# S5 tables planned without a margin, and the scans of an S5 half in two groups with their output products

## The chip, the cores and the metric

The kernel runs on one core of one Trainium2 chip. The metric is device time in microseconds (us). TensorE is called PE here, its weight loads PEld, VectorE DVE, ScalarE ACT, GpSimd POOL and SyncE (which issues the DMAs) SP.

## The reference

Two layers are applied to x, 1024 positions of 1024 channels. Each normalises, projects to nine pieces, runs three mixers on them, gates the result and projects it back:

```
for l in range(DEPTH):                       # DEPTH = 2
    h = rms_norm(x, norm_w[l])
    fq, fk, fv, flog, su, rq, rk, rv, gate = split_cols(h @ w_in[l])
    y_fox = forgetting_attention(fq, fk, fv, log_sigmoid(flog + fox_b_f[l]))
    y_s5  = s5_layer(su, ...)                # 16 groups of 16 channels, 64 complex states
    y_ret = retention(rotary(rq), rotary(rk), rv, ret_gn_w[l])   # 4 heads
    x = x + (concat(y_fox, y_s5, y_ret) * silu(gate)) @ w_out[l]
return rms_norm(x, final_norm_w)
```

The S5 layer is a complex linear recurrence over the positions, x_t = λ x_{t−1} + B u_t, read out by y = Re(C x) + d u, then GELU and a gate. λ and B come from a_re, a_im, b_re, b_im and log_dt by elementwise work on small tables, exp, cos and sin among it.

## The kernel before

PE computes in single precision by three products of split halves (XH·wh, XL·wh, XH·wl), which is why a projection is always a run of 8 + 8 + 8 matmuls of 128x512. Weights arrive as wr; ACT casts them to wh and DVE makes the rest wl.

**S5.** A layer first builds tables (`s5_tables`, `s5_bc`, then `s5_half_tables` for each of two halves of eight groups). PE transposes the rows of a (s5ab) and of c (s5cn); DVE makes powers of λ (s5pw, s5e) and a matrix s5R; PE multiplies s5cc with s5R and transposes s5R, and the results go to DRAM as the matrices s5Bs, s5Cs, s5D and the factors s5Er, s5Ei. Later `s5_half` (L865) works on one half: it loads them and the channels s5U, PE makes Bs·U for two groups of four (ps_s), ACT copies the swapped half out (s5bs, two copies a group), DVE multiplies by Er, POOL the swapped copy by Ei, and DVE subtracts (s5b). Then come eight scans on DVE, s5z along the positions. For the read-out ACT makes swapped copies s5zs, DVE multiplies z by Er, POOL zs by Ei, DVE adds, and PE adds up D·U and Cs·z in ps_s; the GELU follows.

**Retention.** `ret_chain` runs over eight blocks: PE makes scores (ps_s), DVE decays them (rsd) and the state (x), rotated keys are transposed (rkt), PE adds into ps_o, DVE copies to ro. Every two blocks `ret_norm` normalises: ACT squares (rsq), DVE reduces (rvar) and takes an inverse root in small steps (rry, rrt, rrh), scales ro, and PE transposes ro twice two times, which ACT takes out with the weight (ry). The rotation of queries and keys (rot, rsw) is made by ACT copies, two POOL products by cosine and sine, and a DVE sum.

**What sets the order.** The program is written by a planner, the class `Weave`. Each part is a generator thread with a priority and a margin. At `yield need(...)` a thread states what its next step waits for. The planner keeps a clock for PE and takes, in order of priority, the first thread whose inputs are ready, by its own estimate plus the margin, at that clock; it then writes all instructions up to the thread's next `need` into the program. A margin therefore delays a step in PE's order, so that its inputs are surely there. The margins stand in `SLACK` (L29): s5 2.0 us, tab 5.0 us for the tables, rn 3.0, ret 0.5. The order on the other engines is taken by a scheduler that follows this program order and the dependences. Every engine executes its instructions strictly in that order: an instruction that waits holds up all behind it. Every operation is issued through one helper, so the rows of the profile all show its line, L158, and are told apart by their tiles.

PSUM tiles are few: two for projections (ps_proj), three for ps_s, two for ps_t, one for ps_o. A PE step that needs a ps_s waits until the oldest has been read.

`s5_all_tables` (L852) is the thread of the tables; `trunk` adds it for layer 0 at the start, with priority 1, and for layer 1 near the end of layer 0, with priority 5, both with the margin tab.

Of the kernel before, what the change touches and what calls it, by code (L numbers as in the profile page):

```python
# [13 lines left out]
ALU = mybir.AluOpType  # L14
# [14 lines left out]
SLACK = dict(s5=2.0, ret=0.5, rn=3.0, tab=5.0, fox=0.4, val=1.0)  # L29
# [135 lines left out]
def need(*tiles, ps=(), ev=()):  # L165
    return tiles, ps, ev
# [3 lines left out]
def hybrid_block(ctx: ExitStack, tc: tile.TileContext, a: dict, out: bass.AP, taps=None):  # L170
# [4 lines left out]
    W = Weave(PSUM)  # L175
    V, S, G, PE = (Clocked(W, k, e) for k, e in (("V", nc.vector), ("S", nc.scalar), ("G", nc.gpsimd), ("P", nc.tensor)))
# [565 lines left out]
    def s5_bc(l):  # L742

        bb, cc = (slot("pt", [128, 2, 16, 16], F32, n) for n in ("s5bb", "s5cc"))
        B1, B2, C1, C2 = bb[:, 0], bb[:, 1], cc[:, 0], cc[:, 1]
        dma(out=B1[0:64], in_=a["s5_b_re"][l].rearrange("g p h -> p g h"))
        dma(out=B1[64:128], in_=a["s5_b_im"][l].rearrange("g p h -> p g h"))
        V.tensor_scalar(out=B2[0:64], in0=B1[64:128], scalar1=-1.0, scalar2=None, op0=ALU.mult)
        V.tensor_copy(out=B2[64:128], in_=B1[0:64])
        cn = slot("p", [128, 2, 2, 64], F32, "s5cn")  # L750
        for j, nme in enumerate(("s5_c_re", "s5_c_im")):
            dma(out=cn[:, :, j, :], in_=a[nme][l].rearrange("(x g) h p -> (g h) x p", x=2))
        yield need(cn, ps=("t",))
        pt = psum("t", (128, 2, 128))
        for x in range(2):
            PE.transpose(pt[:, x, :], cn[:, x].rearrange("c j p -> c (j p)"), ident)
        V.tensor_copy(out=C1[0:64].rearrange("p (x g) h -> p x (g h)", x=2), in_=pt[0:64])
        V.tensor_scalar(out=C1[64:128].rearrange("p (x g) h -> p x (g h)", x=2), in0=pt[64:128], scalar1=-1.0, scalar2=None, op0=ALU.mult)
        V.tensor_copy(out=C2[0:64], in_=C1[64:128])
        V.tensor_scalar(out=C2[64:128], in0=C1[0:64], scalar1=-1.0, scalar2=None, op0=ALU.mult)  # L760
        return B1, B2, C1, C2
# [90 lines left out]
    def s5_all_tables(l, tag, box, before, mid, hold):  # L852
        yield need(ev=before)
        T = yield from s5_tables(l)
        BC = yield from s5_bc(l)
        box["rho"] = T["rho"]
        W.add(s5_late_tables(l, T, BC), 6)
        yield need(ev=mid)
        for hf in range(2):
            yield from s5_half_tables(l, hf, T, BC, tag, hold[hf])  # L860
            W.done.add(("early", l, hf))

    tanh = [None]

    def s5_half(l, hf, rho):  # L865
        sh = [128, 8, 128]
        tb = tb_d[l, hf]

        def load(j, name):
            t = slot("qb", sh, F32, name)  # L870
            dma(out=t, in_=tb[j])
            return t

        U = slot("qb", sh, F32, "s5U")
        Bs = load(4, "s5Bs")
        dma(out=U, in_=ud_d[hf])
        Er, Ei = load(0, "s5Er"), load(1, "s5Ei")

        D = slot("qb", sh, F32, "s5D")
        kv = kd_d[hf]  # L880
        dma(out=D, in_=bass.AP(kv.tensor, kv.offset, [[16, 8], [1920, 16], [240, 8], [1, 128]]))
        b, bs, z = (slot("p", sh, F32, n) for n in ("s5b", "s5bs", "s5z"))
        for q in range(2):
            gq = slice(q * 4, q * 4 + 4)
            yield need(Bs, U, ps=("s",))
            ps = psum("s", (128, 4, 128))
            for g in range(4):
                PE.matmul(ps[:, g, :], lhsT=Bs[:, q * 4 + g, :], rhs=U[:, q * 4 + g, :], start=True, stop=True)
            S.copy(out=bs[0:64, gq], in_=ps[64:128])
            S.copy(out=bs[64:128, gq], in_=ps[0:64])  # L890
            V.tensor_tensor(out=b[:, gq], in0=ps, in1=Er[:, gq], op=ALU.mult)
            G.tensor_tensor(out=bs[:, gq], in0=bs[:, gq], in1=Ei[:, gq], op=ALU.mult)
            V.tensor_tensor(out=b[:, gq], in0=b[:, gq], in1=bs[:, gq], op=ALU.subtract)
        Cs = load(3, "s5Cs")
        for g in range(8):
            gg = hf * 8 + g
            V.tensor_tensor_scan(out=z[:, g, :], data0=rho[:, gg:gg + 1].to_broadcast([128, 128]), data1=b[:, g, :],
                                 initial=0.0, op0=ALU.mult, op1=ALU.add)
        zs, Y = (slot("p", sh, F32, n) for n in ("s5zs", "s5Y"))
        for q in range(2):  # L900
            gq = slice(q * 4, q * 4 + 4)
            S.copy(out=zs[0:64, gq], in_=z[64:128, gq])
            S.copy(out=zs[64:128, gq], in_=z[0:64, gq])
            V.tensor_tensor(out=z[:, gq], in0=z[:, gq], in1=Er[:, gq], op=ALU.mult)
            G.tensor_tensor(out=zs[:, gq], in0=zs[:, gq], in1=Ei[:, gq], op=ALU.mult)
            V.tensor_tensor(out=z[:, gq], in0=z[:, gq], in1=zs[:, gq], op=ALU.add)
            yield need(z, D, Cs, ps=("s",))
            ps = psum("s", (128, 4, 128))
            for g in range(4):
                gi = q * 4 + g  # L910
                PE.matmul(ps[:, g, :], lhsT=D[:, gi, :], rhs=U[:, gi, :], start=True, stop=False)
                PE.matmul(ps[:, g, 1:128], lhsT=Cs[:, gi, :], rhs=z[:, gi, 0:127], start=False, stop=True)
            S.copy(out=Y[:, gq], in_=ps)

            if q == 0:
                e = slot("p", sh, F32, "s5q")
            S.activation(out=e[:, gq], in_=Y[:, gq], func=AF.Square)
            V.tensor_scalar(out=e[:, gq], in0=e[:, gq], scalar1=0.044715, scalar2=1.0, op0=ALU.mult, op1=ALU.add)
            V.tensor_tensor(out=e[:, gq], in0=e[:, gq], in1=Y[:, gq], op=ALU.mult)
            tanh[0] = S.activation(out=e[:, gq], in_=e[:, gq], func=AF.Tanh, scale=GELU_C)  # L920
            V.scalar_tensor_tensor(out=Y[:, gq], in0=e[:, gq], scalar=1.0, in1=Y[:, gq], op0=ALU.add, op1=ALU.mult)
        dma(out=yd_d[hf], in_=Y)
        W.done.add(("s5h", l))
# [316 lines left out]
    def trunk():  # L1240
        raws = rv_load(0)
        load_x(range(2, NT))
        dma(out=ct, in_=a["c_tab"])
        zt = slot("v", [32, 8, 112], F32, "zt")
        V.memset(zt, 0.0)
        dma(out=kd_d[:, :, :, 0:7, :].rearrange("q c g l h -> (q c) g (l h)"), in_=zt)
        W.add(first_norm(), 0)
        rvw = rv_split(raws, normed[1].ins)
        box = {}
        W.add(s5_all_tables(0, "qb", box, (("xt", 0, 6),), (), ((("su", 0, 1, 0),), (("su", 0, 1, 1),))), 1, SLACK["tab"])  # L1250
        for l in range(depth):
            last = l == depth - 1
            rv = [slot("v", [128, 4, 256], F32, "rv") for _ in range(2)]
            fl = small([128, NT, 8], F32, "fl", 1)
            yield from rv_flog(l, rvw, rv, fl)
            W.add(forget_gates(l, fl), 2)
            U = []
            W.add(s5_chain(l, box), 1, SLACK["s5"])
            W.add(ret_chain(l, U, rv), 2, SLACK["ret"])
            jobs = su_jobs(l, ("qb", "qb") if l else ("qa", "qa")) + rot_jobs(l, U)  # L1260
            for p in range(4):
                tiles = {}
                js = fox_jobs(l, p, tiles)

                def start_k(start=js[3][1], p=p, tiles=tiles):
                    W.add(fox_attend(l, p, tiles), 3)
                    return start()

                jobs += js[:3] + [(js[3][0], start_k, *js[3][2:])]
            c0, c1 = {}, {}  # L1270
            W.add(out_weights(l, 0, c0, (("att", l, 2),)), 4)
            yield from granules(jobs, [gate_job(l, 2), gate_job(l, 3)], [gate_job(l, 0), gate_job(l, 1)])
            src = x_src if l == 0 else x1_d
            W.add(out_weights(l, 1, c1, (("att", l, 3),)), 4)
            if not last:
                box = {}
                W.add(s5_all_tables(l + 1, "qa", box, (("att", l, 3),), (("c0", l),), ((("c1", l, 1),), (("c1", l, 3),))), 5, SLACK["tab"])
            yield from out_first(l, c0, src)
            nw = load_bc("nc", a["final_norm_w"] if last else a["norm_w"][l + 1])
            if not last:  # L1280
                rvw = rv_split(rv_load(l + 1))
            yield from out_second(l, c1, src, nw, last)
# [52 lines left out]
```

## Time and profile before

| | |
|---|---|
| median of three runs | 1197.11 us (1195.18 to 1197.67) |
| the profiled execution | 1195.99 us, its span 1194.3 us |
| PE busy | 1150.3 us, 96% |
| DVE busy | 887.2 us, 74% |
| ACT busy | 543.5 us, 46% |
| POOL busy | 193.6 us, 16% |
| mean granted clock of PE | 0.989 of 2.4 GHz |

The span runs from the first to the last instruction. A granted clock of 1.00 in a stretch is 2.4 GHz; the lower level is 1.2 GHz. In a row of the trace the first number is the start, the second the time from the start of the first to the end of the last instruction of a merged run; brackets hold the idle time of the engine ahead of it and the instruction that ended it. Ends of matmuls overlap the starts of the next, so runs of matmuls are measured from start to start.

### The profile page before, as it was taken

The page shows a single profiled execution, that of the slowest core. Times are in us where ns is not written, and L with a number is a line of the kernel's source. Part 1 is how long each engine was busy: PE and PEld are TensorE (multiplying, and loading weights), DVE is VectorE, ACT ScalarE, POOL GpSimd, SP SyncE. Part 2 cuts the span into 40 slices and gives each one's busy share as a digit, 9 for nine tenths or more (in the row PEclk, how much of TensorE's full clock was granted, in tenths as well). Part 3 has the DMA queues.
Part 4 walks back from the last instruction along what each step waited for, and adds up shares of the span by engine and source line. Part 5 has one row for each costly group of instructions (what it writes and reads, how often), then busy time and mean ns, then how long its engine had stood idle before and what let it go on. Part 6 is the DMA issues. An engine that isn't in the chain of part 4 may idle for free. (4 is left out here: it accounts for less than half of the span.)

```text
span 1194.3 us, 18899 instructions
## 1 busy us (share of the span) xinstructions
PE 1150.3 (96%) x6320; PEld 978.8 (82%) x6320; DVE 887.2 (74%) x2555; ACT 543.5 (46%) x1061; POOL 193.6 (16%) x439
## 2 busy tenths in 40 slices
PE   8899898999999999999999999999999999999997
PEld 7878687878788788987789888877888878898885
DVE  7798886577777678885878938765876868788645
ACT  6436414345555456543243355344544545555312
POOL 0016301121121221200000153111212112121000
PEclk9999999999999999999899999999999999999998
DMA  7157316642405225936241833454352331475524
GB/s 236 40 144 204 109 54 176 168 168 73 122 27 132 73 54 157 305 127 208 90 147 56 256 92 92 112 159 142 115 133 62 89 106 45 133 234 195 181 97 159
DMA packets 147204, 157.44 MB, mean 132 GB/s; under 512 B 20833, under 2 KB 109601, under 8 KB 147106
## 3 DMA queue, kind: packets, MB, share of 16 engines
q1 hardware_dynamic: 147104, 156.22, 44.0%
q8 instruction: 50, 0.82, 0.3%
q14 instruction: 48, 0.39, 0.1%
q10 hardware_dynamic: 2, 0.00, 0.0%
HBM read 99.13 MB, written 40.29 MB: 117 GB/s over the span
## 5 line engine op out<-in xcount | busy, mean ns | idle before, releaser
L158 PE MATMUL ps_proj<-XH,wh 128*128 128x512 f32 (+1 forms) x864 | 228.3, 391 | 4.9 <-DVE ql L158 2.5
L158 PE MATMUL ps_proj<-XL,wh 128*128 128x512 f32 (+1 forms) x864 | 229.7, 391 | 0.0
L158 PE MATMUL ps_proj<-XH,wl 128*128 128x512 f32 (+1 forms) x864 | 223.3, 387 | 0.5 <-DVE wl L158 0.5
L158 PEld LDWEIGHTS ps_proj<-XH,wh 128*128 128x128 f32 x864 | 155.6, 189 | 35.5 <-DVE ql L158 2.9
L158 PEld LDWEIGHTS ps_proj<-XH,wl 128*128 128x128 f32 x864 | 155.8, 188 | 30.3 <-DVE wl L158 1.0
L158 PEld LDWEIGHTS ps_proj<-XL,wh 128*128 128x128 f32 x864 | 156.7, 190 | 28.8
L158 PE MATMUL ps_proj<-wo,XH 128*128 128x512 f32 x512 | 162.8, 393 | 0.0
L158 ACT ACTIVATE P<-P,mn 128x256 f32<-128x256 f32 (+7 forms) x128 | 99.5, 777 | 84.3 <-DVE mn L158 82.9
L158 DVE TENSOR_TENSOR ptl<-ps_t,pth 128x512 fp32r<-128x512 f32 (+1 forms) x160 | 99.5, 632 | 40.7 <-ACT pth L158 39.5
L158 ACT CAST pth<-ps_t 128x512 fp32r<-128x512 f32 (+1 forms) x160 | 85.2, 542 | 80.5 <-PE ps_t L158 57.0
L158 PEld LDWEIGHTS ps_proj<-wo,XH 128*128 128x128 f32 x512 | 95.9, 188 | 19.3
L158 DVE CUSTOM_DVE_ANT_0 P<-ps_s,negc,mn 128x128 f32<-128x128 f32 (+3 forms) x176 | 97.2, 552 | 7.3 <-PE ps_s L158 0.9
L158 PE MATMUL ps_proj<-wo,XL 128*128 128x512 f32 x256 | 100.9, 394 | 0.0
L158 DVE TENSOR_TENSOR wl<-wr,wh 128x1024 fp32r<-128x1024 f32 (+1 forms) x56 | 77.3, 1382 | 23.6 <-PE ps_proj L158 14.5
L158 PE MATMUL ps_t<-ident,P 128*128 128x128 f32 x576 | 84.6, 272 | 0.2
L158 ACT CAST wh<-wr 128x1024 fp32r<-128x1024 f32 (+1 forms) x56 | 66.3, 1188 | 39.3 <-PE ps_proj L158 34.6
L158 POOL TENSOR_SCALAR_AFFINE_SELECT md<-negc 128x128 f32<-128x128 f32 x128 | 43.2, 340 | 178.6 <-DVE mn L158 97.9
L158 PEld LDWEIGHTS ps_t<-ident,P 128*128 128x128 f32 x576 | 67.5, 140 | 5.6 <-DVE P L158 1.0
L158 DVE TENSOR_SCALAR P<-P,rd 128x256 f32<-128x256 f32 (+7 forms) x128 | 67.0, 523 | 2.2
L158 POOL TENSOR_TENSOR rot<-rot,c_cos 128x512 f32<-128x512 f32 x16 | 28.3, 1767 | 237.6 <-ACT rot L158 237.6
L158 PE MATMUL ps_s<-KL,zq 128*128 128x256 f32 (+1 forms) x192 | 65.5, 342 | 0.0
L158 ACT ACTIVATE xs<-xt 128x1024 f32<-128x1024 f32 (+1 forms) x26 | 25.9, 997 | 71.3 <-DVE xt L158 68.3
(253 smaller groups left out, 1983.2 us busy)
## 6 DMA issues: line engine op xcount, KB each, us to landing
wr<-in_w_in_dram SPq DMA_DIRECT2D x56, 512.0 KB, 4.0
negc<-negc_d SPq DMA_DIRECT2D x16, 512.0 KB, 4.4
wor<-in_w_out_dram SPq DMA_DIRECT2D x32, 256.0 KB, 3.6
ys_d<-yt SPq DMA_DIRECT2D x24, 256.0 KB, 2.8
XL<-ys_d SPq DMA_DIRECT2D x8, 768.0 KB, 10.2
XH<-ys_d SPq DMA_DIRECT2D x8, 768.0 KB, 9.8
xt<-x_d SPq DMA_DIRECT2D x24, 256.0 KB, 3.2
TA<-kh SPq DMA_DIRECT2D x32, 128.0 KB, 2.4
```

Of the source, the lines that this page charges most:

```text
L158: r = f(*args, **kw)
```

## The change

Two things. The thread of the tables loses its margin of 5.0 us; the two half tables, which were its last part, become a thread of their own that keeps it. And in `s5_half` the eight scans are written in two groups of four, each behind a `need(b)` and each followed by its own copies and products of the read-out (on ACT, DVE and POOL); the matmuls of the read-out stand in a second loop behind both.

```
 s5_all_tables:
         W.add(s5_late_tables(l, T, BC), 6)
-        yield need(ev=mid)
-        for hf in range(2):
-            yield from s5_half_tables(l, hf, T, BC, tag, hold[hf])
-            W.done.add(("early", l, hf))
+
+        def halves():
+            yield need(ev=mid)
+            for hf in range(2):
+                yield from s5_half_tables(l, hf, T, BC, tag, hold[hf])
+                W.done.add(("early", l, hf))
+
+        W.add(halves(), 5 if l else 1, SLACK["tab"])
...
 s5_half:
         Cs = load(3, "s5Cs")
-        for g in range(8):
-            gg = hf * 8 + g
-            V.tensor_tensor_scan(out=z[:, g, :], data0=rho[:, gg:gg + 1].to_broadcast([128, 128]), data1=b[:, g, :],
-                                 initial=0.0, op0=ALU.mult, op1=ALU.add)
         zs, Y = (slot("p", sh, F32, n) for n in ("s5zs", "s5Y"))
         for q in range(2):
             gq = slice(q * 4, q * 4 + 4)
+            yield need(b)
+            for g in range(q * 4, q * 4 + 4):
+                gg = hf * 8 + g
+                V.tensor_tensor_scan(out=z[:, g, :], data0=rho[:, gg:gg + 1].to_broadcast([128, 128]), data1=b[:, g, :],
+                                     initial=0.0, op0=ALU.mult, op1=ALU.add)
             S.copy(out=zs[0:64, gq], in_=z[64:128, gq])
             S.copy(out=zs[64:128, gq], in_=z[0:64, gq])
             V.tensor_tensor(out=z[:, gq], in0=z[:, gq], in1=Er[:, gq], op=ALU.mult)
             G.tensor_tensor(out=zs[:, gq], in0=zs[:, gq], in1=Ei[:, gq], op=ALU.mult)
             V.tensor_tensor(out=z[:, gq], in0=z[:, gq], in1=zs[:, gq], op=ALU.add)
+        for q in range(2):
+            gq = slice(q * 4, q * 4 + 4)
             yield need(z, D, Cs, ps=("s",))
...
 trunk: both W.add(s5_all_tables(...), 1 or 5, SLACK["tab"]) lose SLACK["tab"]
```

What this does to the order is seen in the program as built. The stretches with another order on PE are, by the times of the trace of before, 44 to 315 us (layer 0), 560 to 620 us (tables of layer 1) and 725 to 1118 us (layer 1).

First place: PE in the tables of layer 0, one piece of the difference. s5ab is the tile with the rows of a, ps_proj_578 the last projection but one of the v and forget-gate columns.

```order
 L158 MATMUL ps_s_571<-ident,xs_470 128x128 x4
-L158 MATMUL ps_proj_578<-wh_174,XH 128x264 x4
+L158 MATMUL ps_proj_578<-wh_174,XH 128x264 x2
+L158 MATMUL ps_t_581<-ident,s5ab_529 128x48
+L158 MATMUL ps_proj_578<-wh_174,XH 128x264 x2
 L158 MATMUL ps_proj_578<-wh_178,XH 128x264 x4
 L158 MATMUL ps_proj_578<-wh_174,XL 128x264 x4
```

The transpose stood at the end of the next such projection, 45 matmuls later.

Second place: DVE in the first S5 half of layer 0. Before (rkt, rsd and x are the retention's):

```order
L158 TENSOR_TENSOR s5b_1346<-ps_s_1531,s5Er_1340 128x512
L158 TENSOR_TENSOR rkt_1571<-ps_t_1568,ct 128x256
L158 TENSOR_TENSOR s5b_1346<-s5b_1346,s5bs_1347 128x512
L158 TENSOR_TENSOR s5b_1346<-ps_s_1541,s5Er_1340 128x512
L158 SCALAR_TENSOR_TENSOR s5z_1348<-s5rho_704,s5b_1346 128x128
L158 TENSOR_TENSOR s5b_1346<-s5b_1346,s5bs_1347 128x512
L158 SCALAR_TENSOR_TENSOR s5z_1348<-s5rho_704,s5b_1346 128x128 x7
```

and after:

```order
L158 TENSOR_TENSOR rot_982<-rot_982,rsw_1426 128x512
L158 TENSOR_TENSOR s5b_1269<-ps_s_1456,s5Er_1263 128x512
L158 TENSOR_TENSOR s5b_1269<-s5b_1269,s5bs_1270 128x512
L158 TENSOR_TENSOR s5b_1269<-ps_s_1466,s5Er_1263 128x512
L158 COPY lfct_1492<-ps_t_1490 64x128
L158 TENSOR_TENSOR s5b_1269<-s5b_1269,s5bs_1270 128x512
L158 SCALAR_TENSOR_TENSOR s5z_1271<-s5rho_656,s5b_1269 128x128 x8
L158 TENSOR_TENSOR rsd_1514<-ps_s_1508,ct 128x2x128
L158 TENSOR_TENSOR rsd_1514<-ps_s_1509,ct 128x2x128
```

The half starts right behind the last rotation (rot_982), ahead of the retention's first scores, whose rsd now stand behind the scans.

Third place: DVE in the second S5 half of layer 1. Before, from the end of a normalisation of ro on (g is a gate, wl weights of a projection):

```order
L158 SCALAR_TENSOR_TENSOR rry_8490<-rrt_8491,rry_8490 128x8
L158 TENSOR_TENSOR ro_8070<-ro_8070,rry_8490 128x512
L158 TENSOR_TENSOR s5b_8270<-ps_s_8551,s5Er_8264 128x512
L158 TENSOR_TENSOR wl_8629<-wr_8626,wh_8628 128x1024
L158 TENSOR_TENSOR s5b_8270<-s5b_8270,s5bs_8271 128x512
L158 TENSOR_TENSOR s5b_8270<-ps_s_8561,s5Er_8264 128x512
L158 SCALAR_TENSOR_TENSOR s5z_8272<-s5rho_6546,s5b_8270 128x128
L158 TENSOR_TENSOR s5b_8270<-s5b_8270,s5bs_8271 128x512
L158 SCALAR_TENSOR_TENSOR s5z_8272<-s5rho_6546,s5b_8270 128x128 x7
L158 SCALAR_TENSOR_TENSOR g_1765_8317<-th_8589,ps_proj_8449 128x512
```

and after:

```order
L158 TENSOR_TENSOR s5b_8226<-s5b_8226,s5bs_8227 128x512
L158 SCALAR_TENSOR_TENSOR rry_8497<-rrt_8498,rry_8497 128x8
L158 TENSOR_TENSOR s5b_8226<-ps_s_8541,s5Er_8220 128x512
L158 TENSOR_TENSOR rrt_8498<-rry_8497 128x8
L158 TENSOR_TENSOR rsd_8568<-ps_s_8562,ct 128x2x128
L158 TENSOR_TENSOR rrt_8498<-rrt_8498,rrh_8499 128x8
L158 TENSOR_TENSOR s5b_8226<-s5b_8226,s5bs_8227 128x512
L158 SCALAR_TENSOR_TENSOR rry_8497<-rrt_8498,rry_8497 128x8
L158 TENSOR_TENSOR rsd_8568<-ps_s_8563,ct 128x2x128
L158 TENSOR_TENSOR ro_8075<-ro_8075,rry_8497 128x512
L158 SCALAR_TENSOR_TENSOR s5z_8228<-s5rho_6529,s5b_8226 128x128 x8
L158 TENSOR_TENSOR ro_8075<-ps_o_8580,ct 128x256
```

The normalisation of ro was done ahead of the S5 products; now it stands behind both subtractions of s5b. In PE's order the first transposes of ro_8075 stand ahead of the next projection now; before, both stood one and a half projections behind it. In the second half of layer 0 the normalised ro_1438 stands in the same way behind the second subtraction and among the scans.

## Rows read from the trace of the kernel before

**Rows 1.** The page, first part: busy time, share of the span, instructions.

```profile
PE 1150.3 (96%) x6320; PEld 978.8 (82%) x6320; DVE 887.2 (74%) x2555; ACT 543.5 (46%) x1061; POOL 193.6 (16%) x439
```

**Rows 2.** Who PE waited for: total us, times, longest us.

```profile
PE ps_t L158 <- DVE s5R L158: 4.3, 2, 2.5
...
PE ps_proj L158 <- DVE ql L158: 2.5, 1, 2.5
PE ps_t L158 <- DVE rkt L158: 2.5, 1, 2.5
PE ps_s L158 <- DVE s5b L158: 1.8, 1, 1.8
PE ps_proj L158 <- DVE g L158: 1.7, 1, 1.7
...
PE ps_o L158 <- DVE ro L158: 1.2, 2, 1.0
PE ps_proj L158 <- ACT rsw L158: 0.7, 1, 0.7
PE ps_s L158 <- DVE s5z L158: 0.5, 1, 0.5
```

**Rows 3.** Stretches: length, busy PE, PEld, DVE, ACT, POOL, granted clock, DMA, GB/s.

```profile
72.00:76.00 4.00, 4.00 (x12) 3.12 (x11) 4.00 (x23) 0.47 (x1) 0.00 (x0) 0.57 0.00 0
...
145.00:155.00 10.00, 6.74 (x26) 5.69 (x27) 10.00 (x24) 3.21 (x6) 2.96 (x2) 0.66 0.20 61
...
206.00:220.00 14.00, 10.94 (x55) 8.80 (x54) 11.88 (x19) 6.08 (x10) 3.27 (x4) 1.00 0.63 158
...
582.00:591.00 9.00, 6.56 (x30) 6.51 (x31) 5.04 (x15) 2.90 (x6) 0.00 (x0) 0.62 0.08 30
...
760.00:785.00 25.00, 23.32 (x147) 20.27 (x146) 21.49 (x52) 10.96 (x18) 6.49 (x4) 1.00 0.27 77
```

**Rows 4.** PE in order of time, tables of layers 0 and 1: start, length.

```profile
50.37 0.26 PE L158 MATMUL ps_t<-ident,s5ab 48*128 48x48 f32 x1
...
69.41 1.96 PE L158 MATMUL ps_t<-s5cc,s5R 128*128 128x16 f32 x16 [1.86 <-DVE s5R L158]
...
563.76 0.26 PE L158 MATMUL ps_t<-ident,s5ab 48*128 48x48 f32 x1
...
584.44 3.57 PE L158 MATMUL ps_t<-s5cc,s5R 128*128 128x16 f32 x16 [2.46 <-DVE s5R L158]
```

**Rows 5.** PE in order of time, first S5 half of layer 0.

```profile
139.64 1.95 PE L158 MATMUL ps_s<-s5U,s5Bs 128*128 128x128 f32 x16
```

**Rows 6.** DVE in order of time, first S5 half of layer 0.

```profile
143.30 1.74 DVE L158 TENSOR_TENSOR s5b<-s5b,s5bs 128x512 f32<-128x512 f32 x1 [0.35 <-POOL s5bs L158]
...
145.90 0.66 DVE L158 TENSOR_TENSOR s5b<-s5b,s5bs 128x512 f32<-128x512 f32 x1
146.48 2.30 DVE L158 TENSOR_TENSOR_SCAN s5z<-s5rho,s5b 128x128 f32<-128x128 f32 x7
...
151.02 1.42 DVE L158 TENSOR_TENSOR s5z<-s5z,s5zs 128x512 f32<-128x512 f32 x1
```

**Rows 7.** POOL in order of time, last rotation and first S5 half, layer 0.

```profile
129.25 2.26 POOL L158 TENSOR_TENSOR rsw<-rsw,c_sin 128x512 f32<-128x512 f32 x1 [1.08 <-ACT rsw L158]
141.97 2.52 POOL L158 TENSOR_TENSOR s5bs<-s5bs,s5Ei 128x512 f32<-128x512 f32 x2 [10.46 <-ACT s5bs L158]
```

**Rows 8.** ACT in order of time, second S5 half of layer 1.

```profile
766.55 0.84 ACT L158 ACTIVATE ry<-ps_t,rgw 128x256 f32<-128x256 f32 x2
...
770.30 2.37 ACT L158 COPY s5bs<-ps_s 64x512 f32<-64x512 f32 x4 [0.28 <-PE ps_s L158]
```

**Rows 9.** PE in order of time, two runs of projection matmuls, layer 1.

```profile
774.42 2.02 PE L158 MATMUL ps_proj<-XL,wh 128*128 128x512 f32 x8
776.28 2.02 PE L158 MATMUL ps_proj<-XH,wl 128*128 128x512 f32 x8
```

**Rows 10.** DVE in order of time, second S5 half of layer 1.

```profile
770.87 0.69 DVE L158 TENSOR_TENSOR ro<-ro,rry 128x512 f32<-128x512 f32 x1
```

More of the change, by code (lines that the diff above doesn't have):

```diff
@@ L1249, in trunk @@
         box = {}
-        W.add(s5_all_tables(0, "qb", box, (("xt", 0, 6),), (), ((("su", 0, 1, 0),), (("su", 0, 1, 1),))), 1, SLACK["tab"])
+        W.add(s5_all_tables(0, "qb", box, (("xt", 0, 6),), (), ((("su", 0, 1, 0),), (("su", 0, 1, 1),))), 1)
         for l in range(depth):
@@ L1276, in trunk @@
                 box = {}
-                W.add(s5_all_tables(l + 1, "qa", box, (("att", l, 3),), (("c0", l),), ((("c1", l, 1),), (("c1", l, 3),))), 5, SLACK["tab"])
+                W.add(s5_all_tables(l + 1, "qa", box, (("att", l, 3),), (("c0", l),), ((("c1", l, 1),), (("c1", l, 3),))), 5)
             yield from out_first(l, c0, src)
```

## The prediction

> **What bounds the kernel now.** I read the page first: TensorE (PE) is busy for 1150.3 us, 96% of the span [rows 1]. A change that moves no matmul work can only move the idle time of PE and the time that it spends at the lower of its two clocks (1.2 instead of 2.4 GHz). Both kernels issue the same 5978 matmuls, so everything below is a balance of waits. The second view is the list of PE's waits [rows 2]: s5R (two waits, 4.3 us), ql, rkt, s5b, g, ro, rsw and s5z all sit in the stretches that the change touches. The third is the table of stretches [rows 3], whose clock column tells which waits were followed by the lower clock. Three were: the wait at 69 us (72:76 at a granted clock of 0.57), the pair in 145:155 (0.66) and the one at 582 us (0.62). The 2.5 us wait for ql in 206:220 and the 1.7 us wait for g in 760:785 were not: both stretches show 1.00.
>
> **What a clock drop costs.** 72:76 is busy throughout, so 4.0 × (1 − 0.57) = 1.7 us are lost. In 582:591, 9.0 × 0.38 = 3.4 us, of which a little lies in the wait: 3.2. In 145:155, 10 × 0.34 = 3.4 us are missing, which is 6.8 us at the lower clock; about 2.1 of these are the wait for rkt, and half of the remaining 4.7 is 2.35 us [rows 3]. For a new drop I take 2.0 us, between 1.7 and 3.2 and nearer to the first, since after a longer wait more of the slow time falls into the wait itself.
>
> **Tables of layer 0 (L0).** Without the margin PE transposes s5ab ahead of the last projection of the previous group, at about 44.8 us instead of 50.37 [rows 4]: 5.6 us earlier. Everything up to s5R hangs on that transpose. In the trace PE stands 1.86 us at 69.41 for s5R [rows 4], and the clock falls behind it. If s5R moves by the same 5.6 us, it is 3.7 us early. Both go: 1.86 + 1.7 = 3.6 us; I take 0.2 back, because DVE must now fit the wl products of the projections between the table steps. **−3.4** (bounds −2.4 and −3.6).
>
> **Tables of layer 1 (L1).** Here s5ab is transposed at about 560.5 us instead of 563.76, and s5cn, which fed the copies that stood between the steps towards s5R, moves up as well. The wait at 584.44 is 2.46 us [rows 4], the drop behind it 3.2. Moved by 3.3 us alone, s5R would be there at 581.1; PE, which asked for it at 582.0, asks 1.6 us earlier in the new order (that much less matmul work stands ahead), at 580.4, and would wait 0.7 us. With s5cn earlier too it would not wait. −5.7 and up to +0.7, of which I take half: **−5.3** (bounds −5.0 and −5.7).
>
> **First S5 half of L0.** In the new order the S5B products stand right behind the last rotated projection, some 15 us earlier than the 139.64 us of the trace [rows 5]: at about 124.8. Gone are the waits for s5b and rkt, 1.77 and 2.47 us [rows 2], with their drop: 4.24 + 2.35 = 6.6. New are waits of the retention scores: rsd_1514 stands on DVE behind all eight scans, and rsd_1542 behind the first group's output product. In the trace that product ends 12.8 us after S5B began (151.02 + 1.42 − 139.64) [rows 5, 6]. At 124.8 the last rotation product, 2.26 us [rows 7], is still ahead on POOL, which holds up s5bs; I put 1.4 of it on the path. So 124.8 + 12.8 + 1.4 + two rsd of 0.4 = 139.8. PE arrives after about 11 us of matmuls: 24 projection matmuls at 8 in 1.9 us [rows 9] are 5.6, S5B 1.8, the scores and transposes the rest. 139.8 − 135.7 = 4.1, in several pieces, the largest near 2.8. With a drop at 0.65 × 2.0 = 1.3: −6.6 + 4.1 + 1.3 = **−1.2** (bounds −3.9, and +1.7 with all of the POOL product and a full drop).
>
> **Second S5 half of L0.** Gone: ro, ql and s5z, 0.97 + 2.52 + 0.54 = 4.0 us [rows 2]; no drop hung on them. New: PE transposes the normalised ro_1438 directly behind the second S5B group. On DVE the normalisation stands behind that group's subtraction, which waits for POOL, which waits for ACT, which waits for those same matmuls. From the end of S5B: two copies s5bs 1.2 [rows 8], POOL 1.26 [rows 7], the subtraction 0.66, two scans 0.66 [rows 6], the last small steps 0.4, ro 0.69 [rows 10], hand-overs 0.3: 5.2 us during which PE has nothing else in its order. The row nearest to the upper bound is the subtraction beside POOL, 1.74 instead of 0.66 [rows 6], and ACT may have two ry ahead (0.84) [rows 8]: 7.1. A wait of 5 us is twice the longest of those that brought the clock down, so 0.95 × 2.0: −4.0 + 5.2 + 1.9 = **+3.1** (bounds +1.2 and +5.1).
>
> **First S5 half of L1.** Same order but for small pieces; the copies of the rotation now stand between those of the first group, and the wait for rsw (0.7) [rows 2] goes. **−0.7** (bounds −0.7 and +0.7).
>
> **Second S5 half of L1.** Gone: g, 1.68 us [rows 2]. New: the same pattern as in L0, and closer. Behind the last product into ps_o, PE has 3.8 us of matmuls (two ro transposes, S5B, one product, four scores) before it transposes ro_8075. Before that ro can be written, ACT makes four ry (1.7) and four s5bs (2.4) [rows 8], POOL the second s5bs (1.26) [rows 7], DVE the subtraction 0.66, rry 0.17, rsd 0.41 and ro 0.69; with the first transpose 0.4 and hand-overs 0.6 that is 8.3 us. 8.3 − 3.8 = 4.5. Then the eight scans, 2.6 us [rows 6], stand before the ro copy that frees ps_o; 1.8 of it is covered by matmuls, so 0.8. Contention of DVE and POOL can add 1.1 once or twice; I take one: 6.4. Drop 1.9: −1.7 + 6.4 + 1.9 = **+6.6** (bounds +3.6 and +7.7).
>
> **The rest.** The attention of L1 is put in another order with the same waits behind it: 0, within ±1.5. The scan split itself adds no instruction and, on DVE, hardly splits anything: in three of the four halves eight scans still stand in a row, so its gain is nil; what it moves is the place of everything else.
>
> **The sum.** −3.4 − 1.2 + 3.1 − 5.3 − 0.7 + 6.6 = −0.9 us. The profiled execution took 1195.99 us, 1.1 below the median of 1197.11; against it the sum gives 1195.1, and from the median 1196.2. I forecast **1195.4**: no change that can be measured (0.2% of the median, 2.4 us, is about what a measurement tells apart: 1194.7 to 1199.5).
>
> **A rule on the clock.** Of the five places with waits above 1.6 us (the pair counted as one) three were followed by 0.57 to 0.66, two by 1.00 [rows 3]. The Trainium skill, TensorE: Matmul & The Clock Gate, section Part 1: The HAM clock gate, says that the throttled state is the default and that activity releases it, at a moment that varies from run to run. By the rule alone all three new waits would end at the lower clock and the sum would be 0.9 us higher; by the rows' share of three in five it would be 1.5 lower.
>
> **Rivals.** (a) *The new waits leave the clock up*, as 206:220 and 760:785 did [rows 3]. The 1.3 + 1.9 + 1.9 go: 1190.3, clearly faster. Against it: the new waits are longer than any of these. Chance 0.25. (b) *DVE and POOL block each other in every group, slower.* The subtraction took 1.74 us beside POOL and 0.66 without [rows 6]: 1.08 more. In the old order one group per half paid it. If the two groups of the three halves that PE waits for all pay, in the input products and again in the output products, that is four to five times 1.08 beyond what is in the sum: 1200. It decides when the two engines' products of one half start within a microsecond of each other. Chance 0.25. The Trainium skill, SBUF — State Buffer, section Who interferes with whom, has it as a rule: a DVE instruction with two SBUF inputs and a POOL instruction that reads SBUF hold a shared port pair in turn, the later one blocked for the whole of the other. The 1.74 against 0.66 agrees; by this rule handing more products to POOL beside DVE saves nothing. (c) *The tables come no earlier in L1*, since DVE also serves the norm of the next layer there. Then half of −5.3 is lost: 1198. For it speaks that DVE's small steps stand between norm steps; against it that both transposes feeding them move up. Chance 0.10.
>
> **Chances.** The forecast holds 0.40, with its own range 1193 to 1198.5; about 0.08 of it lies under 1194.7. Faster: 0.25 + 0.08 = 0.33. Slower: 0.25 from (b) and 0.02 from the edge of (c): 0.27. Same: 0.40. From (a) with short chains to (b) the range is 1188 to 1201.
>
> **What would show it.** Right: no wait for s5R and 1.00 as clock at 70 to 76 and 580 to 591; one wait of 4 to 6 us for ro in each layer's second half, behind DVE's s5b, followed by a clock under 0.7. Wrong: waits for ro under 3 us (then faster), an s5R wait in L1 over 1.5 us, or PE waits in the attention of L1 that the old trace doesn't have.

## The result, and the profile after

The changed kernel takes 1202.45 us (median of six, 1200.59 to 1205.71) against 1197.15 for the kernel before: a ratio of 1.0052, 95% interval [1.0033, 1.0071]. It is slower by half a per cent. The forecast was 1195.4 and no change, with a range up to 1201.

The profiled execution took 1200.59 us, its span is 1198.9. First the page (busy time, share of the span, instructions), to be held against [rows 1], and the list of PE's waits (total us, times, longest us) against [rows 2]:

```profile
PE 1152.8 (96%) x6320; PEld 983.0 (82%) x6320; DVE 889.3 (74%) x2555; ACT 541.4 (45%) x1061; POOL 191.6 (16%) x439
```

```profile
PE ps_t L158 <- DVE ro L158: 11.2, 2, 6.8
...
PE ps_s L158 <- DVE rsd L158: 3.0, 2, 2.3
...
PE ps_t L158 <- DVE P L158: 2.4, 1, 2.4
PE ps_s L158 <- DVE lfe L158: 2.2, 1, 2.2
...
PE ps_s L158 <- DVE s5b L158: 0.9, 1, 0.9
```

The s5R waits of the tables (4.3 us) are gone, and so are ql, rkt and g. In their place stand two waits for ro (11.2 us), two for rsd, one for lfe, and one for P in the attention of layer 1. All idle time of PE, the span less the busy time, has grown by 2.1 us only (46.1 against 44.0), of 4.6 us by which the span is longer. The other 2.5 us are busy time of PE, for the same matmuls; that points to the clock. (The page counts 6320 matmuls in both; the prediction's 5978 are those of the program, some of which the trace shows as two.) The stretches of after (length, busy PE, PEld, DVE, ACT, POOL, granted clock, DMA share, GB/s), to be compared with [rows 3]:

```profile
15.00:24.00 9.00, 6.83 (x34) 6.83 (x35) 8.27 (x28) 3.73 (x9) 0.00 (x0) 0.62 0.83 237
39.00:45.00 6.00, 5.07 (x30) 5.10 (x31) 5.65 (x11) 1.17 (x2) 0.00 (x0) 0.72 0.16 49
...
67.00:77.00 10.00, 9.23 (x51) 7.73 (x50) 10.00 (x42) 2.30 (x4) 0.00 (x0) 1.00 0.73 222
128.00:137.00 9.00, 6.79 (x29) 5.11 (x29) 8.84 (x10) 3.96 (x8) 5.43 (x4) 0.81 0.24 62
145.00:154.00 9.00, 7.21 (x29) 6.07 (x29) 5.17 (x12) 1.79 (x3) 0.25 (x1) 0.62 0.35 118
190.50:194.80 4.30, 0.00 (x0) 0.02 (x1) 4.30 (x16) 0.00 (x0) 0.41 (x1) 0.50 0.26 94
194.80:202.00 7.20, 7.19 (x28) 6.44 (x29) 5.83 (x11) 3.94 (x7) 3.30 (x2) 0.59 0.17 52
582.00:592.00 10.00, 10.00 (x63) 8.74 (x61) 9.86 (x42) 3.78 (x8) 0.00 (x0) 1.00 0.33 101
770.00:779.00 9.00, 4.42 (x23) 4.23 (x24) 7.88 (x20) 3.30 (x6) 2.29 (x3) 0.62 0.13 48
```

The drops behind the two s5R waits are gone (67:77 and 582:592 at 1.00, where before had 0.57 and 0.62). New ones follow the wait for lfe (128:137) and both waits for ro; the one of 145:154 is there in both. Near the start, where PE's order is the same, the drop in 15:24 lasts longer (0.62, where before shows 0.81), and a second one follows in 39:45 (0.72, before 1.00), behind a wait of 2.2 us for xs that both kernels have. The two stretches of before:

```profile
15.00:24.00 9.00, 6.81 (x44) 6.82 (x45) 8.91 (x30) 4.57 (x10) 0.00 (x0) 0.81 0.82 236
39.00:45.00 6.00, 5.00 (x44) 4.82 (x43) 4.46 (x11) 2.15 (x6) 0.00 (x0) 1.00 0.01 3
```

After the wait for ro that ends at 194.8 PE is busy throughout and gets 0.59 of its clock for 7.2 us: 3.0 us lost behind 6.8 us of waiting.

To see where the time went I compare, between points up to which both kernels have done the same matmuls, the length of a stretch less the time that its matmuls take back to back at the full clock. This is PE's lost time, waits and slow clock together. Between the two S5 halves of layer 0 there is no such point, so the sum of their two rows, +7.5, is firmer than either:

| stretch, by what PE does | lost before, us | lost after, us | difference | forecast |
|---|---|---|---|---|
| start, to 44 us | 12.8 | 14.4 | +1.6 | 0 |
| tables of layer 0 | 3.8 | 1.1 | −2.7 | −3.4 |
| first S5 half of layer 0, retention | 9.4 | 12.3 | +2.9 | −1.2 |
| second S5 half of layer 0 | 5.5 | 10.1 | +4.6 | +3.1 |
| attention of layer 0 | 17.5 | 15.3 | −2.2 | 0 |
| tables of layer 1 | 7.2 | 1.4 | −5.8 | −5.3 |
| first S5 half of layer 1 | 2.4 | 1.6 | −0.7 | −0.7 |
| second S5 half of layer 1 | 2.1 | 9.2 | +7.1 | +6.6 |
| rest | 11.5 | 11.3 | −0.2 | 0 |

The sum is +4.6, the difference of the two profiled executions (1200.59 − 1195.99). The median of after lies another 1.9 us above its profiled execution, which was the fastest of the six.

### The profile page after: what moved, and what is told of

The parts are those of the page before. It is cut to its first block, busy times and chain, and to the rows that moved or that the text cites. A ratio compares the mean times of both kernels' runs of the same rounds, so it can differ in the third digit from the quotient of the medians.

```text
span 1198.9 us, 18898 instructions
## 1 busy us (share of the span) xinstructions
PE 1152.8 (96%) x6320; PEld 983.0 (82%) x6320; DVE 889.3 (74%) x2555; ACT 541.4 (45%) x1061; POOL 191.6 (16%) x439
## 4 chain that ended last, share of the span: by engine, by line
PE 49%; DVE 3%; DMA 2%; ACT 1%; issue 1%; DVEq 0%; SPq 0%; ACTq 0%
PE ps_proj L158 36%; PE ps_s L158 5%; PE ps_o L158 4%; PE ps_t L158 4%; DVE P L158 1%; DMA XH<-ys_d 1%; ACT rsw L158 1%; DMA wor<-in_w_out_dram 1%; DVE s5b L158 0%; DVE ptl L158 0%; DMA x_d<-xh 0%; ACT s5zs L158 0%; ACT s5bs L158 0%; DVE x L158 0%; DVE wo L158 0%
```

## The experiments

**The two parts apart.** Three kernels: the tables of layer 1 alone, the tables of both layers alone, the split of the scans alone. They are made from before by these lines of the change (the second W.add of the trunk only; both; none):

```
-        W.add(s5_all_tables(0, "qb", ...), 1, SLACK["tab"])
+        W.add(s5_all_tables(0, "qb", ...), 1)
...
-                W.add(s5_all_tables(l + 1, "qa", ...), 5, SLACK["tab"])
+                W.add(s5_all_tables(l + 1, "qa", ...), 5)
```

> The kernel before with one part of the change alone: the tables of layer 1 lose the margin and the half tables get their own thread. The order of PE differs from before only in the tables of layer 1. Theory A (the table part gains what its waits and clock drop cost, the new waits in the S5 halves and the clock drops behind them lose it): the wait for s5R in layer 1 (2.46 us) and the drop behind it go, 5.8 us less, about 1191.3 us. Theory B (the missing margin itself does harm, the gain does not reach the end because later waits take it up): 1195 to 1197 us.

> The table part of the change in both layers, with the S5 halves written as before. Theory A: layer 0 tables -2.9 us, first S5 half of layer 0 still early with a wait for the forget gate's lfe (2.2 us) and a clock drop, +3.7, layer 1 tables -5.8; no waits of 4 to 7 us for ro: about 1192 us. Theory B: 1197 us or more.

> The split of the scans alone, tables as before. In layer 0 the transposes of ro stand 8 us of matmuls behind the second S5B group, so no long wait for ro there; in layer 1 the order is that of the changed kernel, with the wait for ro behind S5B. Theory A: +7.1 us in layer 1 and about 0 in layer 0, 1203 to 1205 us. Theory B (the split is neutral): 1196 to 1198 us.

In one comparison before took 1198.02 us. Tables of layer 1: 1192.90, ratio 0.9950 [0.9931, 0.9968]; 5.1 us of the 5.8 expected reach the end. Both tables: 1188.75, 0.9915 [0.9897, 0.9933]; better than the 1192 expected. The split alone: 1207.24, 1.0076 [1.0050, 1.0102]; 9.2 us lost where about 7 were expected. Theory A holds for the signs: the tables gain about 9 us, the split loses about as much. But the two don't add up: together they would leave the time where it was, and the change is 5.3 us slower. The long wait for ro in layer 0 explains it in part: only the combination has it. In the trace of the split alone the transposes of ro wait 1.97 us in layer 0 and 4.15 us in layer 1:

```profile
PE ps_t L158 <- DVE ro L158: 6.1, 2, 4.1
```

The trace of the tables alone, its stretches and its waits:

```profile
67.00:77.00 10.00, 10.00 (x55) 8.58 (x55) 9.97 (x38) 3.08 (x5) 0.00 (x0) 1.00 0.87 263
582.00:592.00 10.00, 10.00 (x52) 8.37 (x51) 9.43 (x28) 3.56 (x7) 0.00 (x0) 1.00 0.57 172
```

```profile
PE ps_t L158 <- DVE lfct L158: 3.6, 1, 3.6
...
PE ps_s L158 <- DVE lfe L158: 2.2, 1, 2.2
```

Both table stretches are full. The wait for lfe is there without the split: it belongs to the tables.

**The clock behind the waits.** Does the loss stand in the waits for ro, or in the clock after them? Matmuls on constants fill most of the two waits:

```
         pt = psum("t", (128, 2, 2, 128))
+        if i == 2:
+            for k in range(22 if l == 0 else 15):
+                nc.tensor.matmul(pt[:, k % 2, 0, :], lhsT=ident, rhs=ones, start=True, stop=True)
```

> The changed kernel with 22 (layer 0) and 15 (layer 1) matmuls of 128x128 on constants put in front of the two transposes of ro that wait 6.84 and 4.37 us; their products are overwritten and not used, and they last some 4.9 and 3.3 us, less than the waits. If what is lost behind the waits is the lower clock, the clock stays up, the transposes start as late as before and the time falls by 4 to 5 us to about 1198 us. If the loss is the waits alone, or the drops come from elsewhere, it stays at 1202 us.

It took 1195.70 against 1198.02, 0.9977 [0.9966, 0.9988]: with more matmuls, 0.75% of the time, 9 us, faster than the changed kernel by the two ratios. That is more than the 4 to 5 us expected; the profiled executions lie 4.1 us apart (1196.46 and 1200.59). Its PE in order of time and the stretches, as above:

```profile
187.61 5.08 PE L1099 MATMUL ps_t<-ones,ident 128*128 128x128 f32 x44
194.54 0.66 PE L158 MATMUL ps_t<-ident,ro 128*128 128x128 f32 x4 [1.85 <-DVE ro L158]
```

```profile
186.00:202.00 16.00, 14.15 (x101) 12.91 (x100) 13.49 (x36) 7.10 (x13) 6.21 (x4) 1.00 0.35 104
765.00:780.00 15.00, 13.09 (x88) 11.62 (x89) 12.98 (x30) 4.44 (x8) 4.93 (x4) 1.00 0.26 84
```

The transposes of ro start at 194.54, as they did (194.81); DVE sets that. But the clock stays at 1.00 behind both. So the drops are a loss of their own: in the trace of after they cost 3.0 us behind the first wait and about 1.7 us behind the second, close to what the profiled executions differ by. Where the rest of the 9 us of the medians comes from, no run tells.

**What puts ro there.** In the changed kernel the planner may take another thread at the new `need(b)`; one kernel is without that line, the scans and products still written in groups. A second kernel keeps the line and plans the normalisation of ro later:

```
-            yield need(b)
             for g in range(q * 4, q * 4 + 4):
```

```
-SLACK = dict(s5=2.0, ret=0.5, rn=3.0, tab=5.0, fox=0.4, val=1.0)
+SLACK = dict(s5=2.0, ret=0.5, rn=6.0, tab=5.0, fox=0.4, val=1.0)
```

> The changed kernel without the new line need(b): scans and products are still written in two groups of four, but the planner takes them in one step with the input products of the second group. The transposes of the normalised ro then stand 17 us of matmul work behind the second S5B group in layer 0 and in layer 1, instead of directly behind it. Theory A (the loss is PE's wait for ro behind S5B, with the clock drops after it, and it comes from the planner's break at need(b), not from the split): the waits of 6.84 and 4.37 us and their drops go, 12 to 15 us less than the changed kernel, 1187 to 1190 us. Theory B (the split, by the lock between DVE and POOL, costs the time): 1197 us or more.

> The changed kernel with the margin of the thread that normalises ro at 6.0 instead of 3.0 us, nothing else. The planner puts the transposes of ro at 174.6 instead of 160.0 us of matmul work in layer 0, and none between the S5B groups and the next projection in layer 1. Theory A: both long waits for ro and their clock drops go, 1188 to 1192 us. Theory B: 1200 us or more.

Without `need(b)`: 1189.84 against 1196.93, 0.9939 [0.9921, 0.9956]. With the margin of 6.0: 1182.83, 0.9907 [0.9875, 0.9938]. Theory B is out: both keep the split in groups and both are faster than before. The waits of the second:

```profile
PE ps_s L158 <- DVE rsd L158: 3.0, 2, 2.3
...
PE ps_s L158 <- DVE lfe L158: 2.3, 1, 2.3
```

No long wait for ro is left. Without `need(b)` the long waits for ro are gone too (1.3 us is the longest), but there the S5 products stand ahead of ql on DVE, and PE waits for that:

```profile
202.26 1.22 PE L158 MATMUL ps_proj<-XH,wh 128*128 128x512 f32 x2 [5.28 <-DVE ql L158]
```

**DVE and POOL.** My rival (b) was a mutual block of DVE and POOL. The four products by Ei go to DVE, and the planner is told of a POOL product as before, so that PE's order stays:

```
-            G.tensor_tensor(out=bs[:, gq], in0=bs[:, gq], in1=Ei[:, gq], op=ALU.mult)
+            kw = dict(out=bs[:, gq], in0=bs[:, gq], in1=Ei[:, gq], op=ALU.mult)
+            nc.vector.tensor_tensor(**kw)
+            W.note("G", "tensor_tensor", (), kw)
...                                        # and the same for zs
```

> The changed kernel with the same order on PE, but the four products by Ei of an S5 half are made on DVE instead of POOL. There is nothing left for DVE and POOL to block each other with. If the lock of the two engines makes the waits for ro long, they shorten by 1 to 2 us each and the time falls to 1198 us or less; if it does not, DVE carries 0.66 us more for each product and the time stays at 1201 to 1205 us.

It took 1194.43 against 1196.93, 0.9977 [0.9962, 0.9991], though DVE has eight more products of 0.69 us in each layer. PE's order is the same in both traces. Where POOL was in the way shows in the changed kernel on DVE's small steps towards ro (first fence DVE, second POOL, start and length):

```profile
188.05 0.73 DVE L158 TENSOR_TENSOR rrt<-rry 128x8 f32<-128x8 f32 x1
188.70 0.41 DVE L158 TENSOR_TENSOR x<-ps_s,ct 128x256 f32<-128x256 f32 x1
189.04 0.15 DVE L158 TENSOR_TENSOR rrt<-rrt,rrh 128x8 f32<-128x8 f32 x1
189.11 0.68 DVE L158 TENSOR_TENSOR s5b<-s5b,s5bs 128x512 f32<-128x512 f32 x1
189.71 1.22 DVE L158 SCALAR_TENSOR_TENSOR rry<-rrt,rry 128x8 f32<-128x8 f32 x1
```

```profile
187.49 1.27 POOL L158 TENSOR_TENSOR s5bs<-s5bs,s5Ei 128x512 f32<-128x512 f32 x1 [3.93 <-ACT s5bs L158]
189.54 1.37 POOL L158 TENSOR_TENSOR s5bs<-s5bs,s5Ei 128x512 f32<-128x512 f32 x1 [0.78 <-ACT s5bs L158]
```

The step at 188.05 ends at 188.78, where POOL's product ends (188.76); the one at 189.71 ends at 190.93, where the next one does (190.91). Steps of 0.15 us cost 0.73 and 1.22. The Trainium skill, SBUF — State Buffer, section Who interferes with whom, has the rule: a DVE instruction with two SBUF inputs and a POOL instruction that reads SBUF exclude each other, and the later one is blocked until the first is through. These rows agree; that the block can be many times the blocked step's own 0.15 us is what they add. With the products on DVE the same steps take 0.16, the waits for ro fall from 6.84 to 5.77 and from 4.37 to 3.01 us, and those for rsd from 3.0 to 0.5 in all:

```profile
PE ps_t L158 <- DVE ro L158: 8.8, 2, 5.8
```

The mutual block is real and lengthens the waits. It does not make them: 5.8 and 3.0 us are left without these products on POOL.

**Four more, of which three missed their first figure.** The forget gates were planned later with the table part alone (`W.add(forget_gates(l, fl), 2, 6.0)`):

> The table part alone, with a margin of 6.0 us for the thread of the forget gates, whose small matmuls stood too early for DVE in layer 0 (waits of 2.21 us for lfe and 3.63 us for lfct, two clock drops). PE's order then has them 9.5 us of matmul work later. Expected: 4 to 7 us less than the table part alone (1188.75), 1182 to 1185 us; if the time there is set by the scans that stand ahead of the retention's scores and not by the forget gates, 1187 to 1190.

1188.01 against 1196.93, 0.9931 [0.9909, 0.9953]: no gain over the table part alone (0.9915), the second outcome of the two. The waits for lfe and lfct in layer 0 went, and another took their place at the scores, behind the S5 products on DVE (in layer 1 a wait of 1.8 us for lfct is new):

```profile
135.35 0.71 PE L158 MATMUL ps_s<-rot,rot 64*128 64x128 f32 x6 [3.66 <-DVE s5b L158]
```

Then, in one comparison with before at 1197.13, the margin of 6.0 again, the same margin without the split, and with the products on DVE:

> The changed kernel with the margin of 6.0 us for the normalisation of ro, once more, on the same chip as the next two. If its 1182.8 us was no luck: 1182 to 1187 us.

> The same margin of 6.0 us with the table part alone, the S5 halves written as before. It tells whether the split of the scans gives anything once the waits for ro are away. If the split is worth something where the order is good, this is slower than the changed kernel with the same margin, 1187 to 1190 us; if the split gives nothing, the two are within 2 us.

> The changed kernel with the margin of 6.0 us and the products by Ei on DVE instead of POOL; PE's order is that of the changed kernel with the margin. In the first half of layer 0 the waits for rsd (0.74 and 2.29 us) stood behind products that DVE shared with POOL; if these are what made them, they go and the time falls by 2 to 4 us to 1179 to 1182 us; if DVE is the limit there, it stays at 1183 us or rises.

The changed kernel with the margin took 1185.06, 0.9898 [0.9883, 0.9913]. The same margin without the split took 1195.59, 0.9982 [0.9972, 0.9992], more than expected, and by the ratios 0.7% more than the tables without it (0.9915). At the start of the attention of layer 0 a new order makes PE wait for mn, rd, P and ptl, and the clock falls; it loses 8 us there in waits and clock, where the tables with the margin of 3.0 wait 2.4 us:

```profile
308.00:323.00 15.00, 9.66 (x48) 7.30 (x46) 12.57 (x33) 7.84 (x15) 2.37 (x6) 0.77 0.55 158
```

So the 10 us between the two are for the most part not a worth of the split; about 6 of them are what this one order costs. With the products on DVE: 1176.69, 0.9825 [0.9808, 0.9841], better than expected and the best of all. Its stretches at the places of the S5 halves:

```profile
111.00:137.00 26.00, 23.77 (x109) 19.32 (x107) 25.30 (x47) 13.99 (x24) 10.43 (x7) 0.93 0.47 130
137.00:154.00 17.00, 16.53 (x114) 13.92 (x114) 16.57 (x53) 6.07 (x10) 0.00 (x0) 1.00 0.26 88
...
186.00:222.00 36.00, 36.00 (x181) 30.17 (x180) 19.71 (x46) 15.51 (x26) 3.44 (x7) 1.00 0.65 172
...
760.00:785.00 25.00, 25.00 (x131) 21.15 (x130) 14.63 (x34) 11.46 (x20) 3.57 (x7) 1.00 0.68 185
```

PE is full there, but for the wait for lfe.

## Why the prediction was wrong, point by point

**What bounds, and where.** Right: no matmul work moved, and the balance is of waits and of the clock. The places were the right ones too, but for the start and the attention of layer 0. Between the forecast −0.9 and the +4.6 of the profiled executions lie 5.5 us: 4.1 in the first S5 half of layer 0, 1.5 in the second, 1.6 at the start, and −2.2 from the attention of layer 0; the other rows about cancel.

**Tables.** Right in mechanism and size: −2.7 and −5.8 us in the traces for −3.4 and −5.3; tables alone, −9.3 us in the medians.

**Second half of layer 1.** Right: +7.1 for +6.6, with a wait for ro of 4.37 (4.5 forecast), small ones before and after it, and the drop.

**Second half of layer 0.** The mechanism was right, the size was not: 6.84 us of waiting for a term of 5.2, though inside its bound of 7.1, and a drop of 3.0 for 1.9. (The prediction took 2.0 us for a drop because more of the slow time would fall into a longer wait; the longest wait was followed by one of the costliest drops.) The chain was summed from undisturbed steps. Two of the small steps, which the sum had at 0.4 together, were blocked by POOL for 1.65 us more.

**First half of layer 0: the step that failed.** Forecast −1.2, measured +2.9. The waits for rsd came to 3.0 us, with lfct 3.5, for a term of 4.1; that was right. But I followed only S5B as it moved, and not the forget gate's matmuls, which moved up by 6.5 us of matmul work and now stand right behind S5B. DVE had not made lfe yet: a wl of 1.22 us stands between its last steps, and the last one ends at 131.09, where POOL's rotation product ends (131.07). The rows of DVE and of PE in the changed kernel:

```profile
126.64 2.14 DVE L158 TENSOR_TENSOR lfe<-lfe,lf 128x8 f32<-128x8 f32 x6
128.72 1.22 DVE L158 TENSOR_TENSOR wl<-wr,wh 128x1024 fp32r<-128x1024 f32 x1
129.86 1.23 DVE L158 TENSOR_TENSOR lfe<-lfe,lf 128x8 f32<-128x8 f32 x1
```

```profile
131.15 0.43 PE L158 MATMUL ps_s<-lfe,ones 128*128 128x64 f32 x2 [2.21 <-DVE lfe L158]
```

That is 2.2 us and a drop of 9.0 × 0.19 = 1.7 us, for which the sum had no term. And the drop behind the wait for rsd, weighed at 1.3, missed 9.0 × 0.38 = 3.4 us of clock, of which about 3.1 fell on matmuls. These are 5.7 us more than forecast, 1.6 more than the row shows; the shorter waits for rsd and lfct are 0.6 of that. Part of it is the luck of one execution: the kernel with a margin of 6.0 has the same order on PE up to here and the same wait for rsd, 2.29 us, and of its two profiles one shows no lower clock behind it and the other does:

```profile
143.00:152.00 9.00, 6.71 (x48) 5.61 (x46) 6.57 (x14) 2.31 (x4) 0.97 (x1) 1.00 0.33 118
```

```profile
143.00:152.00 9.00, 6.84 (x35) 5.76 (x35) 5.46 (x12) 1.79 (x3) 0.62 (x1) 0.81 0.37 118
```

**Drops.** In the S5 halves the forecast paid 5.1 us for three. There were four, at 1.7, about 3, 3.0 and about 1.7 us. All four waits were followed by the lower clock, so for this execution the prediction's larger count, all of them, was nearer than the three in five of [rows 3]. But the new wait of 2.41 us for P left the clock up, as one profile above did behind rsd. The share itself was counted over the stretches of the change only: the full list of before has three more waits above 1.6 us, for ms (2.6, followed by 0.81 in 15:24), for xs (2.2, 1.00 in 39:45) and for x (1.7, without a drop). With them it is four of eight.

**The start.** Forecast 0; 1.6 us were lost ahead of any change in PE's order. The range had no term for it. In 15:24 after has 9.0 × (0.81 − 0.62) = 1.7 us less at the full clock, in 39:45 another 6.0 × 0.28 = 1.7; a little shorter waits and slow time that fell into waits give part of it back. The difference begins earlier: the same four matmuls at 12.9 us ran faster in after, so PE came sooner to the wait for ms, which DVE ends at the same time in both (first fence before, second after):

```profile
12.89 1.23 PE L158 MATMUL ps_proj<-wh,XH 128*128 128x264 f32 x4 [0.21 <-ACT XH L158]
...
17.19 1.09 PE L158 MATMUL ps_proj<-wh,XL 128*128 128x264 f32 x4 [2.58 <-DVE ms L158]
```

```profile
12.88 0.79 PE L158 MATMUL ps_proj<-wh,XH 128*128 128x264 f32 x4 [0.21 <-ACT XH L158]
...
17.17 1.25 PE L158 MATMUL ps_proj<-wh,XL 128*128 128x264 f32 x4 [3.02 <-DVE ms L158]
```

The order on PE and on DVE is the same up to there. Of the profiles of all kernels eight have a wait of 2.3 to 2.9 us here and show 0.81 in 15:24, four a wait of 3.0 to 3.1 and 0.62; one has no record of the clock. The drop in 39:45 differs between two profiles of one kernel, the margin of 6.0: 0.75 and 1.00. So the 1.6 us look like a chance of the execution and not like a cost of the change; more profiles of one kernel would have to show it.

**The attention of layer 0** gave 2.2 us back, all but 0.2 of it where the order on PE is unchanged. The forecast had no such term; why, no run tells.

**The rivals.** (a) is out for this execution: all four new waits in the S5 halves were followed by the lower clock. Elsewhere a new wait did leave it up, the one for P in the attention of layer 1:

```profile
1079.65 0.98 PE L158 MATMUL ps_t<-ident,P 128*128 128x128 f32 x7 [2.41 <-DVE P L158]
```

```profile
1070.00:1085.00 15.00, 11.58 (x79) 9.56 (x78) 13.19 (x48) 8.59 (x24) 4.03 (x14) 1.00 1.09 354
```

The prediction had named such a wait as a sign that it is wrong. The sign came, but this part took no longer in all (the row "rest", −0.2). (b) had the right end, slower, and the right effect between DVE and POOL, but not its place: the long products of the halves are blocked about as often as before; it is the small steps that pay. (c) is out: the s5R wait in layer 1 is gone. The claim that the split itself gains nothing is not contradicted: with POOL's products in place the best order with the split (0.9898 and 0.9907) is not clearly faster than the tables alone (0.9915), and the products on DVE were not tried without the split. That the split moves everything else was the larger part.

## What to carry to other kernels

When a step moves in the order of the bounding engine, list all that moves with it and look up when each input is written, not only the inputs of the step that has the name. Price a chain of small steps beside another engine by its blocked rows. Give every new wait of two microseconds or more a chance of the slow clock behind it; here four of five had it in one execution, for 1.7 to 3.1 us each. Where a wait can't be avoided, matmuls on constants in it may be worth more than they cost. A margin in a planner is neither waste nor gain by itself: taken from the tables it gave 9 us, added to the normalisation it gave 17 us in the changed kernel and cost 0.7% with the tables alone.

## What the runs showed of the hardware that I had not expected

A DVE instruction of 128x8 elements, 0.15 us when alone, took 0.73 and 1.22 us beside a POOL product and ended with it to 0.02 us. Eight products a layer moved from POOL to DVE, the busier engine, made the kernel 0.75% faster by the two ratios (1.0052 and 0.9977), and 8.4 us faster in one comparison with a good order (1185.06 to 1176.69). And the same wait of 2.29 us for rsd, in two profiles of one kernel, was followed by a granted clock of 1.00 in the one and 0.81 in the other.
